# A windowed attention mixer in two-unit steps: keys' low halves laid out twice, weights divided by their sum before the transposes, two query chunks moved behind the values

## The chip, the core and the metric

One NeuronCore of a Trainium2 chip runs the kernel. TensorE (PE) multiplies, VectorE (DVE) and ScalarE (ACT) work elementwise and read the products from PSUM, GpSimd (POOL) works elementwise on SBUF and issues some of the transfers, SyncE (SP) issues the rest. The metric is the device time in microseconds of one execution, median of the runs.

## What is computed

Four layers with mixers A, B, C, A over 256 latent and 256 context tokens of width 1024, each mixer followed by a squared-ReLU MLP. The change is in mixer B, windowed grouped-query attention with 16 query heads, 4 key heads, head width 64. Latent queries see latent keys within 128 tokens and all context keys; context queries see context keys alone. The softmax has a learned sink logit per head:

```
def sink_softmax(scores, sink):
    m = sink
    for s in scores:
        m = jnp.maximum(m, jnp.max(s, axis=-1))
    ps = [jnp.exp(s - m[..., None]) for s in scores]
    denom = jnp.exp(sink - m)
    for p in ps:
        denom = denom + jnp.sum(p, axis=-1)
    return [p / denom[..., None] for p in ps]
```

## The kernel before

Activations are feature-major, eight chunks of 128 features by 512 tokens (latent first), in `h`, and split for matmuls into a high and a low half, `xh` and `xl`. Weights come as 374 blocks of 128x1024 in a fixed order; each is loaded by SP into a ring of four (`raw`), split by ACT (line 240) and DVE (line 245) into a ring of five (`hl`), and multiplied in three passes (`mm3`, lines 375 to 377). `w_get(ahead)` takes the next block and first queues the splits of the next `ahead` blocks on ACT and DVE. The order on every engine is that of the program text; the framework adds the waits.

Mixer B makes two key chunks and eight query chunks (`chunk`, `evac`, `put`, `rotate`), then the values for all heads (`v_step`, 256 columns, token-major), then attends. A unit is 128 queries of two heads (hh 0 and 1), that is a tuple (G, blk, j); there are 32, in groups of four (j) over blocks 0, 2, 1, 3: four latent units against 512 keys, four context units against 256, and so on. Latent units are called L, context units C below. A loop step `attend(x)` issues

- `s1(x)`: scores, two passes with the keys' high halves over 128 rows (line 1271), two with the low halves over 64 rows (line 1275), and for L a window mask of 256 columns per head (line 1278);
- `s4(x-2)`: transposes of the exponentials, 128x128 each (line 1331), and the copy to SBUF by ACT (line 1333), into `h`, whose contents are saved in DRAM meanwhile;
- `over_sum(x-2)`: a product of ones with a diagonal of the reciprocal sums (line 1352), which spreads them along a row;
- `pv(x-3)`: products with the values, two column halves of 64 (line 1343);
- `s2(x)`: row maxima (lines 1292, 1297), exponentials with row sums (line 1314), sums, reciprocals, diagonals.

At the end of a block `block_end` multiplies the outcome by the spread reciprocals (line 1364) and splits it into `xh`, `xl` (lines 1321, 1322). Eight output chunks follow: the first halves of chunks 0 and 1 are drawn into the last steps, 2 to 4 go through `chunk` with the default `ahead=4`, and 5 to 7 are the tail that `transition` multiplies between the mixer and the MLP (it takes their weights by `w_get(0)`). After each output chunk the residual is added (line 550) and its square taken for the norm (line 444).

Of the kernel before, what the change touches and what calls it, by code (L numbers as in the profile page):

```python
# [19 lines left out]
T = 256  # L20
DEPTH = 4
HID = 4096
NK = 8
# [52 lines left out]
def weight_order():  # L76

    order = []
    for l in range(DEPTH):
# [127 lines left out]
class Body:  # L207
# [968 lines left out]
    def mixer_b(self, l, i):  # L1176
        nc, tc = self.nc, self.tc
        with ExitStack() as st:
# [3 lines left out]
            KL = [bp.tile([128, 512], F32R, name=f"KL{G}") for G in range(2)]  # L1182
# [30 lines left out]
            def rotate(u, o):  # L1213
# [3 lines left out]
                def rest():  # L1217
                    rp = self.aux()[:, 0:T]
# [33 lines left out]
            S, P, PT, rsum, esum, diag = {}, {}, {}, {}, {}, {}  # L1252
            outs = [self.bank() for _ in range(4)]

            ring = [self.bank(), self.bank()]
            ring += [self.aux(), self.aux()]
            po, pr = outs[2], outs[3]
# [4 lines left out]
            def s1(x):  # L1262
# [5 lines left out]
                ss = [ring[2 * (x % 2) + hh] for hh in range(2)]  # L1268
                qs = Q2[G * 4 + j]
                for hh in range(2):  # L1270
                    nc.tensor.matmul(ss[hh][:, :nk], lhsT=qs[hh][:, ts_], rhs=K2[2 * G + hh][:, k0:512], start=True, stop=False)  # L1271

                for hh in range(2):
                    rows = slice(64 * hh, 64 * hh + 64)
                    nc.tensor.matmul(ss[hh][:, :nk], lhsT=qs[hh][rows, ts_], rhs=KL[G][rows, k0:512], start=False, stop=not lat)
                if lat:
                    for s in ss:
                        nc.tensor.matmul(
                            s[:, 0:T], lhsT=self.ident16, rhs=self.mask_w[:, blk * T : blk * T + T], start=False, stop=True
                        )  # L1280
                S[x] = [s[:, :nk] for s in ss]

            def s2(x):

                if x < N:
                    G, blk, j = units[x]
                    ci = G * 4 + j
                    nsk = self.nsinks[:, ci * 2 : ci * 2 + 2]
                    ngm = bq.tile([128, 2], F32, tag="ngm", name="ngm", bufs=4)
                    es = esum[x] = bq.tile([128, 2], F32, tag="es", name="es", bufs=4)  # L1290
                    rs = rsum[x] = bq.tile([128, 2], F32, tag="rs", name="rs", bufs=4)
                    nc.vector.tensor_reduce(ngm[:, 0:1], S[x][0], axis=AX.X, op=ALU.max, negate=True)
                old = rsum.get(x - 1)
                if x >= 1 and old is not None:
                    nc.vector.tensor_tensor(out=old, in0=old, in1=esum[x - 1], op=ALU.add)
                if x < N:
                    nc.vector.tensor_reduce(ngm[:, 1:2], S[x][1], axis=AX.X, op=ALU.max, negate=True)
                if old is not None:
                    nc.vector.reciprocal(old, old)
                if x < N:  # L1300
                    nc.vector.tensor_tensor(out=ngm, in0=ngm, in1=nsk, op=ALU.min)
                if old is not None:
                    diag[x - 1] = [bq.tile([128, 128], F32, tag="diag", name="diag", bufs=6) for _ in range(2)]
                    nc.vector.tensor_scalar(diag[x - 1][0], self.ident, old[:, 0:1], None, op0=ALU.mult)
                if x < N:
                    nc.vector.tensor_tensor(out=es, in0=ngm, in1=nsk, op=ALU.subtract)
                if old is not None:
                    nc.vector.tensor_scalar(diag[x - 1][1], self.ident, old[:, 1:2], None, op0=ALU.mult)
                if x < N:
                    P[x] = []  # L1310
                    for hh in range(2):
                        p = bq.tile([128, 512], F32, tag="p", name="p", bufs=6)
                        nk = S[x][hh].shape[-1]
                        nc.scalar.activation(
                            p[:, :nk], S[x][hh], AF.Exp, bias=ngm[:, hh : hh + 1], accum_out=rs[:, hh : hh + 1]
                        )
                        P[x].append(p[:, :nk])
                    nc.scalar.activation(es, es, AF.Exp)
                if block_done:
                    xh, xl, t = block_done.pop()  # L1320
                    nc.scalar.copy(xh, t)
                    nc.vector.tensor_tensor(out=xl, in0=t, in1=xh.bitcast(F32), op=ALU.subtract)

            def s4(x):
                G, blk, j = units[x]
                nkc = len(keys_of(blk)[0])
                PT[x] = []
                for hh in range(2):
                    tp = outs[hh].rearrange("p (c t) -> p c t", c=4)
                    for c in range(nkc):  # L1330
                        nc.tensor.transpose(tp[:, c, :], P[x][hh][:, c * 128 : c * 128 + 128], self.ident)  # L1331
                    t = self.h[:, 2 * (x % 4) + hh, :].rearrange("p (c t) -> p c t", c=4)
                    nc.scalar.copy(t[:, :nkc, :], tp[:, :nkc, :])
                    PT[x].append(t)

            def pv(x):
                G, blk, j = units[x]
                kcs = keys_of(blk)[0]
                js = slice(j * 128, j * 128 + 128)
                for c, kc in enumerate(kcs):  # L1340
                    for hh in range(2):
                        g = 2 * G + hh
                        nc.tensor.matmul(  # L1343
                            po[64 * hh : 64 * hh + 64, js], lhsT=vv[:, kc, g * 64 : g * 64 + 64], rhs=PT[x][hh][:, c, :],
# [3 lines left out]
            def over_sum(x):  # L1348

                j = units[x][2]  # L1350
                for hh in range(2):
                    nc.tensor.matmul(
                        pr[64 * hh : 64 * hh + 64, j * 128 : j * 128 + 128], lhsT=self.ones[:, 0:64], rhs=diag[x][hh],
                        start=True, stop=True,
                    )
# [379 lines left out]
```

## Time and profile before

| | |
|---|---|
| median of 3 runs | 2121.88 us (2120.83 to 2123.21) |
| profiled execution, its own time | 2119.28 us |
| its span, first to last instruction | 2117.4 us |
| PE busy | 2065.0 us, 98% |
| DVE, ACT, POOL busy | 1443.7, 950.7, 85.8 us |
| mean granted clock of PE | 0.993 |

A row of a timeline gives the start and the length of one instruction or of several merged ones. Matmuls are pipelined, so the length of one is longer than the distance to the next; what a group costs PE is read from the start of the next group. Mean durations of DVE and ACT are of single instructions.

### The profile page before, as it was taken

How to read it: one execution, taken by the hardware profiler on the slowest of the kernel's cores; microseconds unless marked ns; L12 is line 12 of the kernel's file. 1: busy time of each engine (PE TensorE's matmuls, PEld its weight loads, DVE VectorE, ACT ScalarE, POOL GpSimd, SP SyncE). 2: the span in 40 equal slices, each digit the busy share in tenths (PEclk: the TensorE clock that was granted, in tenths of full speed). 3: DMA queues.
4: the chain of work that ended last, by engine and by line, in shares of the span. 5: the costliest groups of instructions: out<-in, count | busy, mean ns of one | idle time of the engine just before them, and what ended most of it. 6: DMA issues, size and time to landing. Idle time of an engine off the chain costs nothing.

```text
span 2117.4 us, 30418 instructions
## 1 busy us (share of the span) xinstructions
PE 2065.0 (98%) x11782; PEld 1751.1 (83%) x11782; DVE 1443.7 (68%) x2636; ACT 950.7 (45%) x1818; POOL 85.8 (4%) x143
## 2 busy tenths in 40 slices
PE   6998999999999999999999999999999999989998
PEld 3667798888889877988888888898888889879997
DVE  5657777787767776677777664467777766577554
ACT  3426654324235585624234342362423435556554
POOL 0113100000000000000000000000000000310000
PEclk9999999999999999999999999999999999999999
DMA  9784235555553103255565333235556533635552
GB/s 297 266 283 113 75 128 174 186 189 179 188 171 118 52 1 130 90 189 180 180 197 177 122 110 100 90 110 189 183 179 195 181 110 110 174 98 186 182 185 92
DMA packets 97025, 326.11 MB, mean 154 GB/s; under 512 B 17760, under 2 KB 18928, under 8 KB 96240
## 3 DMA queue, kind: packets, MB, share of 16 engines
q1 hardware_dynamic: 80464, 291.19, 42.7%
q0 software_dynamic: 15872, 32.46, 5.0%
q8 instruction: 92, 1.51, 0.3%
q10 hardware_dynamic: 544, 0.52, 0.1%
q14 instruction: 53, 0.43, 0.1%
HBM read 319.73 MB, written 4.33 MB: 153 GB/s over the span
## 4 chain that ended last, share of the span: by engine, by line
PE 94%; DVE 3%; ACT 2%; DMA 1%; issue 1%; POOL 0%; DVEq 0%; SPq 0%; ACTq 0%
PE bank L375 25%; PE bank L377 25%; PE bank L376 25%; PE bank L576 2%; PE bank L577 2%; PE bank L579 2%; PE bank L407 2%; PE bank L409 1%; PE bank L408 1%; PE bank L291 1%; PE bank L1331 1%; PE bank L1343 1%; PE bank L1271 1%; DVE wlo L245 1%; ACT rb L942 1%; PE bank L1008 1%
## 5 line engine op out<-in xcount | busy, mean ns | idle before, releaser
L375 PE MATMUL bank<-xh,whi 128*128 128x512 f32 (+1 forms) x1600 | 578.8, 362 | 2.5 <-ACT h L895 1.8
L240 ACT CAST whi<-raw 128x1024 fp32r<-128x1024 f32 x374 | 387.1, 1044 | 419.9 <-PE bank L376 382.8
L376 PE MATMUL bank<-xl,whi 128*128 128x512 f32 (+1 forms) x1600 | 573.6, 358 | 0.2
L377 PE MATMUL bank<-xh,wlo 128*128 128x512 f32 (+1 forms) x1600 | 573.4, 358 | 0.0
L245 DVE TENSOR_TENSOR wlo<-raw,whi 128x1024 fp32r<-128x1024 f32 x374 | 454.8, 1223 | 165.6 <-ACT whi L240 165.0
L338 DVE SCALAR_TENSOR_TENSOR junk<-ada,cbc 128x1024 bf16<-128x1024 f32 x312 | 380.9, 1221 | 6.8 <-DMA ada<-in_ada 2.5
L375 PE MATMUL bank<-hh,whi 128*128 128x512 f32 (+1 forms) x1096 | 384.5, 351 | 0.0
L376 PE MATMUL bank<-hl,whi 128*128 128x512 f32 (+1 forms) x1096 | 383.9, 350 | 0.0
L377 PE MATMUL bank<-hh,wlo 128*128 128x512 f32 (+1 forms) x1096 | 383.9, 350 | 0.0
L375 PEld LDWEIGHTS bank<-xh,whi 128*128 128x128 f32 x1600 | 304.5, 190 | 53.3 <-issue 4.7
L376 PEld LDWEIGHTS bank<-xl,whi 128*128 128x128 f32 x1600 | 304.4, 190 | 43.8 <-DVE xl L928 1.0
L377 PEld LDWEIGHTS bank<-xh,wlo 128*128 128x128 f32 x1600 | 304.2, 190 | 44.0
L376 PEld LDWEIGHTS bank<-hl,whi 128*128 128x128 f32 x1096 | 207.4, 189 | 27.4
L375 PEld LDWEIGHTS bank<-hh,whi 128*128 128x128 f32 x1096 | 207.4, 189 | 27.3
L377 PEld LDWEIGHTS bank<-hh,wlo 128*128 128x128 f32 x1096 | 207.4, 189 | 27.0
L550 DVE SCALAR_TENSOR_TENSOR h<-bank,mod,h 128x256 f32<-128x256 f32 x280 | 125.6, 480 | 142.3 <-PE bank L377 142.2
L661 DVE TENSOR_TENSOR hl<-q,hh 128x512 fp32r<-128x512 f32 (+1 forms) x137 | 81.5, 595 | 170.4 <-ACT q L660 170.1
L658 ACT ACTIVATE r<-bank 128x512 f32<-128x512 f32 (+1 forms) x137 | 70.8, 517 | 268.9 <-PE bank L377 266.0
L444 ACT ACTIVATE sq<-h 128x256 f32<-128x256 f32 (+1 forms) x74 | 36.0, 487 | 140.9 <-DVE h L550 115.7
L576 PE MATMUL bank<-xh,whi 128*128 128x256 f32 x312 | 81.6, 290 | 3.5 <-ACT xh L512 3.5
L577 PE MATMUL bank<-xh,wlo 128*128 128x256 f32 x312 | 80.2, 285 | 0.0
L659 ACT ACTIVATE hh<-r 128x512 fp32r<-128x512 f32 (+1 forms) x137 | 75.9, 554 | 4.6
(269 smaller groups left out, 2144.0 us busy)
## 6 DMA issues: line engine op xcount, KB each, us to landing
raw<-in_wts SPq DMA_DIRECT2D x374, 512.0 KB, 4.2
ada<-in_ada SPq DMA_DIRECT2D x156, 512.0 KB, 3.5
first<-in_ada POOLq DMA_DIRECT2D x17, 512.0 KB, 5.1
start<-in_ada SPq DMA_DIRECT2D x16, 512.0 KB, 8.8
cbc<-line POOLq DMA_DIRECT2D x4, 1024.0 KB, 8.5
rb<-dnm POOLq DMA_DIRECT2D x16, 256.0 KB, 6.6
ab<-dar POOLq DMA_DIRECT2D x16, 256.0 KB, 10.8
h<-in_hin SPq DMA_DIRECT2D x4, 512.0 KB, 7.8
```

The source lines that it names most:

```text
L240: self.nc.scalar.copy(hi, self.raw[j])
L245: self.nc.vector.tensor_tensor(out=lo, in0=self.raw.pop(j), in1=hi.bitcast(F32), op=ALU.subtract)
L338: nc.vector.scalar_tensor_tensor(out=junk, in0=w, scalar=1.0, in1=self.cbc[:, s, :], op0=ALU.mult, op1=ALU.mult, accum_out=self.mods[l][:, ...
L375: mm(out, lhsT=whi, rhs=xhi, start=first, stop=False)
L376: mm(out, lhsT=whi, rhs=xlo, start=False, stop=False)
L377: mm(out, lhsT=wlo, rhs=xhi, start=False, stop=last)
L550: self.nc.vector.scalar_tensor_tensor(out=self.h[:, m, a:b], in0=o[:, a - sl.start : b - sl.start], scalar=mod[:, gate + m, s : s + 1], in ...
L576: mm(o[:, :T], lhsT=w[0][:, c], rhs=hi[:, sl], start=(k == 0), stop=False)
L577: mm(o[:, :T], lhsT=w[1][:, c], rhs=hi[:, sl], start=False, stop=False)
L658: nc.scalar.activation(r[:, :n], o, AF.Relu)
L659: nc.scalar.activation(hh[:, sl], r[:, :n], AF.Square)
L661: nc.vector.tensor_tensor(out=hl[:, sl], in0=q[:, :n], in1=hh[:, sl].bitcast(F32), op=ALU.subtract)
```

## The change

A loop step now holds two units of the same block, a pair `y` with units `2y` and `2y+1`, 16 pairs in all.

- The keys' low half lies at both halves of the rows (`KL[g]`), so that all score products use 128 rows. The mask is added on the 128 columns where it isn't zero.
- `maxima` takes both heads of a unit in one reduction; the sink's term is made once for a pair.
- `normalise` adds the sums, takes reciprocals, and has GpSimd multiply the exponentials by them, in place, ahead of the transposes. The diagonals, `over_sum` and the multiplication in `block_end` are gone.
- `turn` transposes with a ring of three banks; of an L unit ACT copies head 0 and DVE head 1, of a C unit DVE copies both at once.
- `pv` multiplies the values with both units of a pair, 256 columns.
- Query chunks 8 and 9 are multiplied behind the values, one before the loop and one in its step 1.
- Five output chunks instead of two have their first halves in the last steps, their second halves follow, and the tail of three is handed on at once. `h` comes back in two transfers.

The bodies that go stand in the listing above and are left out of the diff, as are lines that only move:

```diff
-            order += [("colq", "b_w_qkv", i, m) for m in range(8)]
+            order += [("colq", "b_w_qkv", i, m) for m in range(6)]
             order += [("mov", "b_w_qkv", i, 1280, 256, kk) for kk in range(2)]
+            order += [("colq", "b_w_qkv", i, m) for m in range(6, 8)]
             order += [("rowq", "b_w_out", i, m) for m in range(8)]
...
-            KL = [bp.tile([128, 512], F32R, name=f"KL{G}") for G in range(2)]
+            KL = [bp.tile([128, 512], F32R, name=f"KL{g}") for g in range(4)]
...
                     if u < 2:
                         hi = K2[2 * u + hh]
-                        lo = KL[u][rows, sl]
+                        lo = KL[2 * u + hh]
                         nc.scalar.copy(hi[away, sl], src[rows])
+                        parts.append((rows, hi[rows, sl], lo[rows, sl]))
+                        parts.append((rows, hi[rows, sl], lo[away, sl]))
                     else:
-                        lo = hi[away, sl]
+                        parts.append((rows, hi[rows, sl], hi[away, sl]))
                     nc.scalar.activation(hi[rows, sl], src[rows], AF.Copy, scale=scale)
-                    parts.append((rows, hi[rows, sl], lo))
...
-                def rest():
-                    rp = self.aux()[:, 0:T]
+                def rest(bank=None):
+                    rp = (self.aux() if bank is None else bank)[:, 0:T]
...
-            for u in range(3, 10):
+            for u in range(3, 8):
                 self.chunk(u, self.x_chunk, ALL, evac)
...
+            N = len(units) // 2
+            bk = self.banks
+            tring, po = [bk[2], bk[4], bk[3]], bk[5]
+            S, P, sums = {}, {}, {}
+            tpos = [0]
...
                 nk = 512 - k0
                 ts_ = slice(blk * 128, blk * 128 + 128)
                 lat = blk < 2
+                at = 6 * (x % 2)
+                ss = self.allb[:, at : at + 2, 0:nk]
                 qs = Q2[G * 4 + j]
                 for hh in range(2):
+                    g = 2 * G + hh
+                    nc.tensor.matmul(ss[:, hh, :], lhsT=qs[hh][:, ts_], rhs=K2[g][:, k0:512], start=True, stop=False)
+                    nc.tensor.matmul(ss[:, hh, :], lhsT=qs[hh][:, ts_], rhs=KL[g][:, k0:512], start=False, stop=not lat)
+                if lat:
+                    c = (1 - blk) * 128
+                    for hh in range(2):
+                        nc.tensor.matmul(
+                            ss[:, hh, c : c + 128], lhsT=self.ident16, rhs=self.mask_w[:, blk * T + c : blk * T + c + 128],
+                            start=False, stop=True,
+                        )
+                S[x] = ss
+            def maxima(x):
+                G, blk, j = units[x]
+                y, a = divmod(x, 2)
+                if a == 0:
+                    sums[y] = [bq.tile([128, 4], F32, tag=t, name=t, bufs=4) for t in ("ngm", "es", "rs")]
+                ngm = sums[y][0]
+                c = slice(2 * a, 2 * a + 2)
+                ci = G * 4 + j
+                nc.vector.tensor_reduce(ngm[:, c], S[x], axis=AX.X, op=ALU.max, negate=True)
+                nc.vector.tensor_tensor(out=ngm[:, c], in0=ngm[:, c], in1=self.nsinks[:, 2 * ci : 2 * ci + 2], op=ALU.min)
+                if a == 1:
+                    nc.vector.tensor_tensor(
+                        out=sums[y][1], in0=ngm, in1=self.nsinks[:, 2 * ci - 2 : 2 * ci + 2], op=ALU.subtract
+                    )
+            def exps(x):
+                y, a = divmod(x, 2)
+                ngm, es, rs = sums[y]
+                P[x] = []
                 for hh in range(2):
+                    p = bq.tile([128, 512], F32, tag="p", name="p", bufs=8)
+                    nk = S[x].shape[-1]
+                    at = 2 * a + hh
+                    nc.scalar.activation(
+                        p[:, :nk], S[x][:, hh, :], AF.Exp, bias=ngm[:, at : at + 1], accum_out=rs[:, at : at + 1]
+                    )
+                    P[x].append(p[:, :nk])
+                if a == 1:
+                    nc.scalar.activation(es, es, AF.Exp)
+            def normalise(y):
+                ngm, es, rs = sums.pop(y)
+                nc.vector.tensor_tensor(out=rs, in0=rs, in1=es, op=ALU.add)
+                nc.vector.reciprocal(rs, rs)
+                for a in range(2):
                     for hh in range(2):
+                        p = P[2 * y + a][hh]
+                        nc.gpsimd.tensor_scalar(p, p, rs[:, 2 * a + hh : 2 * a + hh + 1], None, op0=ALU.mult)
+            def turn(x):
+                nk = len(keys_of(units[x][1])[0]) * 128
+                at = 2 * (x % 4)
+                ps = P.pop(x)
+                if nk == 512:
+                    for hh in range(2):
+                        tp = tring[tpos[0] % 3]
+                        tpos[0] += 1
+                        for c in range(0, nk, 128):
+                            nc.tensor.transpose(tp[:, c : c + 128], ps[hh][:, c : c + 128], self.ident)
+                        if hh == 0:
+                            nc.scalar.copy(self.h[:, at, :], tp)
+                        else:
+                            nc.vector.tensor_copy(self.h[:, at + 1, :], tp)
+                else:
+                    tp = tring[tpos[0] % 3].rearrange("p (a k) -> p a k", a=2)
+                    tpos[0] += 1
+                    for hh in range(2):
+                        for c in range(0, nk, 128):
+                            nc.tensor.transpose(tp[:, hh, c : c + 128], ps[hh][:, c : c + 128], self.ident)
+                    nc.vector.tensor_copy(self.h[:, at : at + 2, 0:nk], tp)
+            def pv(y):
+                G, blk, j = units[2 * y]
                 kcs = keys_of(blk)[0]
+                at = 4 * (y % 2)
                 for c, kc in enumerate(kcs):
                     for hh in range(2):
                         g = 2 * G + hh
                         nc.tensor.matmul(
+                            po[64 * hh : 64 * hh + 64, j * 128 : j * 128 + 256], lhsT=vv[:, kc, g * 64 : g * 64 + 64],
+                            rhs=self.h[:, at + hh : at + hh + 3 : 2, c * 128 : c * 128 + 128],
                             start=(c == 0), stop=(c == len(kcs) - 1),
                         )
+            def block_end(y):
+                G, blk, _ = units[2 * y]
+                sl, cs = slice(blk * 128, blk * 128 + 128), slice(G * 4, G * 4 + 4)
+                t = po.rearrange("p (j t) -> p j t", j=4)
+                nc.scalar.copy(self.xh[:, cs, sl], t)
+                nc.vector.tensor_tensor(out=self.xl[:, cs, sl], in0=t, in1=self.xh[:, cs, sl].bitcast(F32), op=ALU.subtract)
+            early = []
+            def begin(o):
+                early.append((self.w_get(-1), o))
+                self.unit(o, early[-1][0], self.x_chunk, ALL, range(4))
+            def query(u, o, between, ahead):
+                w = self.w_get(ahead)
+                self.unit(o, w, self.x_chunk, ALL, range(4))
+                between()
+                self.unit(o, w, self.x_chunk, ALL, range(4, NK))
+                evac(u, o, ALL)
+            vo = [bk[j] for j in (5, 4, 3, 2)]
             for kk in range(2):
                 w = self.w_get(3 - kk)
                 for kx in range(4):
+                    self.v_step(w, 4 * kk + kx, vo, 256)
                     if pend and kx in (0, 2):
                         pend.pop(0)()
                     if kk == 1 and kx % 2 == 1:
                         s1(kx // 2)
             for tcn in range(4):
+                nc.scalar.copy(vv[:, tcn, :], vo[tcn][:, 0:256])
             for x in range(2):
+                maxima(x)
+                exps(x)
+            query(8, bk[5], lambda: None, 2)
+            for y in range(1, N + 3):
+                if y >= 5 and y % 2 == 1:
+                    block_end(y - 4)
+                t = 2 * (y - 2)
+                if 2 <= y < N + 2:
+                    turn(t)
+                if y < N:
+                    s1(2 * y)
+                    maxima(2 * y)
+                if y <= N:
+                    normalise(y - 1)
+                if y == 1:
+                    query(9, bk[4], lambda: pend.pop(0)(bk[2]), 3)
+                if y == 2:
+                    pend.pop(0)(bk[3])
+                if y in (N, N + 1):
+                    begin(bk[6 * (y - N)])
+                if 2 <= y < N + 2:
+                    turn(t + 1)
+                if y < N:
+                    exps(2 * y)
+                    s1(2 * y + 1)
+                    maxima(2 * y + 1)
+                    exps(2 * y + 1)
+                if y in (N, N + 1):
+                    begin(bk[6 * (y - N) + 1])
+                if y >= 3:
+                    pv(y - 3)
+                if y in (N - 3, N - 1):
                     self.wsplit_to(self.wsplit + 1)
+                if y > N:
+                    c = slice(4 * (y - N - 1), 4 * (y - N - 1) + 4)
+                    nc.gpsimd.dma_start(out=self.h[:, c, :], in_=saved[:, c, :])
+            begin(bk[2])
+            block_end(N - 1)
         res = self.residual(l, 16, 512)
         for m, (w, o) in enumerate(early):
             self.unit(o, w, self.x_chunk, ALL, range(4, NK))
             res(m, o, ALL)
+        self.bpos = 3
         yield self.x_chunk, res, (5, 6, 7)
```

## Rows read from the trace of the kernel before

**Rows 1.** The page's part 4, the chain that ended last, by engine

```profile
PE 94%; DVE 3%; ACT 2%; DMA 1%; issue 1%; POOL 0%; DVEq 0%; SPq 0%; ACTq 0%
```

**Rows 2.** PE in order of time: start us, us, engine, line, tiles, count

```profile
742.11 0.66 PE L1331 MATMUL bank<-cons,p 128*128 128x128 f32 x4
...
742.97 0.61 PE L1343 MATMUL bank<-h,vv 128*64 128x128 f32 x8
743.51 0.73 PE L1271 MATMUL bank<-K,Q 128*128 128x512 f32 x2
...
751.91 0.73 PE L1271 MATMUL bank<-K,Q 128*128 128x512 f32 x2
...
753.01 0.39 PE L1278 MATMUL bank<-mask_w,ident 128*128 128x256 bf16 x2
753.24 1.04 PE L1331 MATMUL bank<-cons,p 128*128 128x128 f32 x8
754.21 0.44 PE L1352 MATMUL bank<-diag,ones 128*64 128x128 f32 x4
754.48 1.04 PE L1343 MATMUL bank<-h,vv 128*64 128x128 f32 x16
755.45 0.51 PE L1271 MATMUL bank<-K,Q 128*128 128x256 f32 x2
...
756.20 1.09 PE L1331 MATMUL bank<-cons,p 128*128 128x128 f32 x8
...
766.20 0.73 PE L1271 MATMUL bank<-K,Q 128*128 128x512 f32 x2
```

**Rows 3.** PE in order of time, where the transition follows the output chunks

```profile
843.37 0.39 PE L377 MATMUL bank<-xh,wlo 128*128 128x512 f32 x1
843.59 0.28 PE L375 MATMUL bank<-xh,whi 128*128 128x256 f32 x1
843.71 0.28 PE L376 MATMUL bank<-xl,whi 128*128 128x256 f32 x1
```

**Rows 4.** Groups by line and form, 716 to 822 us: count | busy us, mean ns | idle before

```profile
L1314 ACT ACTIVATE p<-bank,ngm 128x512 f32<-128x512 f32 x32 | 21.7, 683 | 6.2 <-DVE ngm L1301 5.1
L1333 ACT COPY h<-bank 128x512 f32<-128x512 f32 x32 | 17.1, 592 | 0.6 <-PE bank L1331 0.6
L1314 ACT ACTIVATE p<-bank,ngm 128x256 f32<-128x256 f32 x32 | 15.0, 478 | 3.1 <-DVE ngm L1301 2.3
L1292 DVE TENSOR_REDUCE ngm<-bank 128x1 f32<-128x512 f32 x16 | 11.0, 687 | 3.1 <-PE bank L1278 3.1
L1292 DVE TENSOR_REDUCE ngm<-bank 128x1 f32<-128x256 f32 x16 | 6.8, 423 | 6.1 <-PE bank L1275 5.7
```

**Rows 5.** DVE and ACT in order of time: the hand-over to an exponential

```profile
746.99 0.16 DVE L1301 TENSOR_TENSOR ngm<-ngm,nsinks 128x2 f32<-128x2 f32 x1
...
747.24 0.69 ACT L1314 ACTIVATE p<-bank,ngm 128x512 f32<-128x512 f32 x1 [1.34 <-DVE ngm L1301]
```

**Rows 6.** POOL and DVE in order of time, in mixer A of layer 0

```profile
156.87 1.29 POOL L875 TENSOR_TENSOR ab<-ab,qT 128x512 f32<-128x512 f32 x1
...
177.83 1.60 POOL L875 TENSOR_TENSOR ab<-ab,qT 128x512 f32<-128x512 f32 x1
...
177.62 0.68 DVE L901 SCALAR_TENSOR_TENSOR h<-h,ssum 128x512 f32<-128x512 f32 x1
178.34 1.65 DVE L902 SCALAR_TENSOR_TENSOR h<-h,ssum 128x512 f32<-128x512 f32 x1
```

**Rows 7.** Groups of POOL, whole span, shapes apart

```profile
L806 POOL MEMSET wrow<- 40x512 f32 x2 | 1.2, 594 | 0.0
```

**Rows 8.** The page's part 5, costliest groups of the whole span

```profile
L240 ACT CAST whi<-raw 128x1024 fp32r<-128x1024 f32 x374 | 387.1, 1044 | 419.9 <-PE bank L376 382.8
...
L245 DVE TENSOR_TENSOR wlo<-raw,whi 128x1024 fp32r<-128x1024 f32 x374 | 454.8, 1223 | 165.6 <-ACT whi L240 165.0
...
L550 DVE SCALAR_TENSOR_TENSOR h<-bank,mod,h 128x256 f32<-128x256 f32 x280 | 125.6, 480 | 142.3 <-PE bank L377 142.2
```

More of the change, by code (lines that the diff above doesn't have):

```diff
@@ L1267, in s1 @@
                 lat = blk < 2
-                ss = [ring[2 * (x % 2) + hh] for hh in range(2)]
+                at = 6 * (x % 2)
+                ss = self.allb[:, at : at + 2, 0:nk]
                 qs = Q2[G * 4 + j]
                 for hh in range(2):
-                    nc.tensor.matmul(ss[hh][:, :nk], lhsT=qs[hh][:, ts_], rhs=K2[2 * G + hh][:, k0:512], start=True, stop=False)
-                for hh in range(2):
-                    rows = slice(64 * hh, 64 * hh + 64)
-                    nc.tensor.matmul(ss[hh][:, :nk], lhsT=qs[hh][rows, ts_], rhs=KL[G][rows, k0:512], start=False, stop=not lat)
@@ L1276, in s1 @@
[L1276 to L1310, printed above, removed]
-                    for hh in range(2):
[L1312 to L1334, printed above, removed]
@@ L1343, in pv @@
                         nc.tensor.matmul(
-                            po[64 * hh : 64 * hh + 64, js], lhsT=vv[:, kc, g * 64 : g * 64 + 64], rhs=PT[x][hh][:, c, :],
+                            po[64 * hh : 64 * hh + 64, j * 128 : j * 128 + 256], lhsT=vv[:, kc, g * 64 : g * 64 + 64],
+                            rhs=self.h[:, at + hh : at + hh + 3 : 2, c * 128 : c * 128 + 128],
                             start=(c == 0), stop=(c == len(kcs) - 1),
                         )
[L1348 to L1355, printed above, removed]
-                if j == 3:
-                    t = bq.tile([128, 512], F32, tag="on", name="on", bufs=2)
-                    nc.scalar.copy(t, pr)
-                    over.append(t)
@@ L1361, in block_end @@
-            def block_end(G, blk):
-                sl = slice(blk * 128, blk * 128 + 128)
-                t = over.pop()
-                nc.vector.tensor_tensor(out=t, in0=po, in1=t, op=ALU.mult)
-                cs = slice(G * 4, G * 4 + 4)
-                block_done.append((self.xh[:, cs, sl], self.xl[:, cs, sl], t.rearrange("p (j t) -> p j t", j=4)))
-            N = len(units)
-            over, block_done, early = [], [], []
-            def attend(x):
-                if x >= 7 and x % 4 == 3:
-                    block_end(*units[x - 4][:2])
-                if x < N:
-                    s1(x)
-                if 2 <= x < N + 2:
-                    s4(x - 2)
-                    over_sum(x - 2)
-                if 3 <= x < N + 3:
-                    pv(x - 3)
-                s2(x)
+            def block_end(y):
[4 more added lines that the diff above has]
+                nc.vector.tensor_tensor(out=self.xl[:, cs, sl], in0=t, in1=self.xh[:, cs, sl].bitcast(F32), op=ALU.subtract)
@@ L1391, in mixer_b @@
             for tcn in range(4):
-                nc.scalar.copy(vv[:, tcn, :], outs[tcn][:, 0:256])
+                nc.scalar.copy(vv[:, tcn, :], vo[tcn][:, 0:256])
             for x in range(2):
-                s2(x)
-            for x in range(2, N + 4):
-                attend(x)
-                if x in (N, N + 2):
-                    self.wsplit_to(self.wsplit + 1)
-                if x in (N + 1, N + 2):
-                    early.append((self.w_get(-1), ring[x - N - 1]))
-                    self.unit(early[-1][1], early[-1][0], self.x_chunk, ALL, range(4))
-            for c in range(0, 8, 2):
-                nc.gpsimd.dma_start(out=self.h[:, c : c + 2, :], in_=saved[:, c : c + 2, :])
+                maxima(x)
[30 more added lines that the diff above has]
+                if y in (N - 3, N - 1):
+                    self.wsplit_to(self.wsplit + 1)
+                if y > N:
[3 more added lines that the diff above has]
+            block_end(N - 1)
         res = self.residual(l, 16, 512)
@@ L1408, in mixer_b @@
             res(m, o, ALL)
-        for m in range(2, 5):
-            self.chunk(m, self.x_chunk, ALL, res)
+        self.bpos = 3
         yield self.x_chunk, res, (5, 6, 7)
```

9 lines of the change are left out of this document (removed).

## The prediction

> **What bounds the kernel now.** I read the chain that ended last first: 94% of it is PE [rows 1], so what PE is given to do counts, and so does each moment in which it has to wait. Then PE's timeline inside mixer B [rows 2]. The distance from one group's start to the next is its price. An L unit: scores 1.33 us (751.91 to 753.24, of which the mask pair is 0.23), eight transposes 0.97, the spread sums 0.27, values 0.97; in all 3.54. A C unit: scores 0.75 (755.45 to 756.20), four transposes and spread sums together 0.86 (742.11 to 742.97), so 0.59 for the transposes, values 0.54; in all 2.15. Four of each are 22.8, and the trace has 22.7 from one block of L units to the next (743.51 to 766.20): no time is lost in a round, PE sets its pace, and there are four rounds. Last, the groups of DVE and ACT in that stretch [rows 4], for what each step costs on the engines that must follow.
>
> **The change, PE's work first.** A pass of 512 columns on the whole array is 0.22, one of 256 is 0.12 [rows 3]. New scores of an L unit are four passes and half the mask, 0.88 + 0.12 = 1.0, of a C unit 4 x 0.12 = 0.48. Transposes stay, 0.97 and half of that, 0.49. The spread sums go. Value products are half as many with twice the columns: at most what they were, 1.94 for an L pair and 1.08 for a C pair; at least half of that, if columns cost nothing. I take the first, since columns are what PE streams in rows 3. So an L pair is 2 x 1.0 + 2 x 0.97 + 1.94 = 5.9 instead of 7.1, a C pair 0.96 + 0.98 + 1.08 = 3.0 instead of 4.3, a round 17.8 instead of 22.7. Over four rounds PE has 19.6 less to do (27 with the other end of the value price).
>
> **Whether PE can run at 17.8.** A round asks 17.8 of DVE and 13.6 of ACT by the prices below, so at best DVE just keeps up. And each engine takes its instructions in order, so I followed the order. DVE prices: a reduction is 0.69 for 512 columns and 0.42 for 256, so 1.22 for the 1024 that two heads now are; a copy of 512 columns from PSUM or the subtraction of `block_end` the same 0.69; a [128,2] operation 0.16 [rows 5]. ACT: a copy 0.59, exponentials of a unit 2 x 0.68 or 2 x 0.48 [rows 4]; a hand-over to ACT 0.1 (746.99 + 0.16 to 747.24) [rows 5]. From PE to a reader I take 0.2, the 0.28 of a matmul less the 0.12 between two [rows 3]. One round, from the last exponential of step 4 to that of step 8:
>
> - Step 5 (second L pair, C transposes): ACT's cast of `block_end` stands behind the exponentials of step 4, DVE's subtraction waits for it and stands first on DVE. 0.59 + 0.69, copy 0.69, maxima 1.38, sum and reciprocal 0.32, copy 0.69, maxima 1.38, hand-over 0.1, exponentials 1.36: 7.2.
> - Step 6 (C scores, L transposes): three banks take four transposes, so the last waits for ACT's copy of the first, and that copy is behind step 5's exponentials. Copy 0.59, transposes 0.49, scores 0.48, 0.2, maxima 0.85, 0.1, exponentials 0.96: 3.7.
> - Steps 7 and 8: cast 0.59, copy 0.59 and the transposes that wait for its bank 0.49, scores 0.48, values 1.94, next transposes 0.49, L scores 1.0, 0.2, maxima 1.38, sum and reciprocal 0.32, copy 0.69, maxima 1.38, 0.1, exponentials 1.36: 11.0.
>
> That is 21.9 a round, with PE waiting 4.1 of it; DVE and ACT then hold most of the gain. Against 22.7 it saves 0.8, and over 3.5 rounds (the first half round is the filling) 2.8.
>
> **GpSimd's products.** Four per pair; the trace has no product with a scalar there. Below it costs the 0.59 of a fill of 512 columns that reads nothing [rows 7], above the 1.29 of a product with two inputs [rows 6]; it reads one tensor, so I take the middle, 0.9. In step 5 the sums are ready some 3.5 into the 7.2; two products end 1.8 later, before the bank is free, and the fourth at 7.1, just before it is wanted. At 0.9 the price is nothing and the cover is that bank wait; at 1.29 the fourth comes 1.5 later, and step 7 meets the same again: up to 2 a round. The page "GPSIMD Engine Reference" of the Trainium skill, on the side-by-side cycle accounting, has 769 ns for 512 elements in its best loop with one input; by that figure the sum would be the same and the slow GpSimd below less likely. No row here shows it.
>
> **A port that two engines share.** Alone, DVE's operation on two SBUF tensors took 0.68; the next of that shape took 1.65, and a POOL product ran from 177.83 to 179.43, 0.56 ahead of DVE's end at 179.99 [rows 6], so DVE's own work began when the product was done. So they exclude each other. The new `min` and `subtract` on `ngm` and `nsinks` read two SBUF tensors, and the `min` of the second unit of each step falls among the four products. Waiting half a product each time costs 2 x 0.45 for L products and 2 x 0.25 for C: 1.4 a round at most, none if so small an operation slips in or the wait is off the chain. Behind the waiting `min` stand the exponentials, for which the scores' banks and the next sums wait. I take half, 0.7 a round, 2.5 in all. The Trainium skill, "SBUF — State Buffer", section Who interferes with whom, says that the shared pair is an exclusive lock and that the loser blocks for the whole instruction; the trace agrees with 1.65 against 0.68. By the rule the sum would be 2.4 higher, without it 2.5 lower.
>
> **Filling.** Query chunk 9 is evacuated on ACT ahead of the exponentials of unit 2, and its rotation is put into the bank that unit 1's transposes want, with DVE's read behind sums that wait for unit 3's exponentials. I count 4.5 of PE waiting in steps 2 and 3. Half a round of the work removed (2.4) and the old filling and draining waits, which five output halves now cover, go against it: 0 in the sum, -2 to +3.
>
> **The split in step 13.** `wsplit_to` puts a cast of 1.04 on ACT and a subtraction of 1.22 on DVE [rows 8], between the step's exponentials and the copies of L transposes of step 14. DVE waits there for the cast. Both lie on the chain: 2.3, and 2.9 with the fourth GpSimd product late; I take 2.5. If the chain has slack, 0. The one in step 15 meets output products that cover it.
>
> **The tail.** Before, PE went from the output chunks into the transition without a gap (843.37, 843.59, 843.71) [rows 3], since chunks 2 to 4 had queued the splits of 5 to 7. Now no `w_get` between step 15 and the transition splits ahead, and ACT and DVE take the split of output block 5 behind the residual and square of chunk 4. After its last matmul: 0.2, two residuals 0.96, a square 0.6 (as an ACT pass of 512), cast 1.04, subtraction 1.22: 4.0 during which PE has at most two passes to do. Nothing covers it.
>
> **Costed at nothing.** The moved query chunks are the same 48 passes of 512 each. The keys' second low half is eight more DVE passes of 0.42 under query products; 3.4 without that cover. The mask on fewer columns is in the scores. The return of `h` is issued a step before its first reader, with half chunks of 12 x 0.22 = 2.6 between; it comes into the tail's wait one for one if it lands later than three of them. SP's queue has loaded its four blocks long before, and the moved blocks keep their order there.
>
> **Sum.** -2.8 + 2.5 + 0 + 2.5 + 4.0 = +6.2. On the profiled execution's 2119.3 that is 2125.5; the median of the runs lies 2.6 above that, so 2128.
>
> **Rivals.**
> - *PE keeps its pace of 17.8.* Decided where the chain of steps 5 to 8 takes less than 17.8 instead of 21.9. For it: the sums of DVE and ACT would just allow it, and a chain worked out by hand is easily too long by a hand-over here and there. Against: the order of the text makes step 5's chain, and three banks make step 6's. Then -19.6, the split covered, the tail paid: -15.6, 2106. Half way between, 20 a round: -9.5 + 1 + 2.5 + 4.0 = -2, and -5.5 without port waits and split (2116).
> - *It cancels.* No port waits and a chain shorter by 1: 6.2 - 2.5 - 3.5 = 0, 2122. Nothing in the trace excludes it; both terms are estimates.
> - *GpSimd is slow.* Products at 1.29 add 2 a round: +7, 2135; with the port held from one product to the next, a `min` waits for several: up to 2142. For it: the one product that the trace has costs 1.29; against: it reads twice as much.
>
> **How the numbers follow.** About 0.2% (4.2) is what a measurement here can tell from no change. Forecast (+4.2 to +13): 0.37. Slow GpSimd: 0.14. Cancels, -4.2 to +4.2: 0.23. PE at its pace or half way: 0.26. So slower 0.51, same 0.23, faster 0.26. The range leaves out the full pace at the one end (about 0.1) and the worst of GpSimd at the other: 2109 to 2139; the likeliest case alone is 2125 to 2134.
>
> **What would show it.** Right, if a round of eight units is 21 to 23.5 long with PE waiting several us in it, on banks that ACT's copies free and on GpSimd's products; if `min` of [128,2] has long instances beside GpSimd's products; if PE stands still about 4 before the transition, behind a cast and a subtraction. Wrong, if rounds are near 18, if GpSimd's product is over 1.2 or under 0.6, or if score passes over 128 rows with repeated weights don't come at 0.22.

## The result, and the profile after

The changed kernel takes 2146.12 us (median of 4 runs, 2141.96 to 2148.44) against 2122.55 of the kernel before (4 runs): 1.0109 times, 95% interval [1.0097, 1.0122], some 23.6 us slower. Forecast were 2128, within 2109 to 2139: the sign held, the size didn't. The profiled execution is the slowest of the four (2148.44; span 2146.7). The chain that ended last, from its page, answers to [rows 1], with GpSimd's product on it. The last line is that product's group, two shapes mixed:

```profile
PE 89%; DVE 5%; ACT 2%; POOL 2%; issue 1%; DMA 1%; SPq 0%; DVEq 0%; ACTq 0%; POOLq 0%
PE bank L376 24%; PE bank L378 24%; PE bank L377 24%; POOL p L1326 2%; PE bank L577 2%; PE bank L578 2%; PE bank L580 2%; PE bank L408 2%; PE bank L410 1%; PE bank L409 1%; PE bank L292 1%; DVE wlo L246 1%; ACT rb L943 1%; PE bank L1009 1%; PE bank L1358 1%
...
L1326 POOL TENSOR_SCALAR p<-p,rs 128x512 f32<-128x512 f32 (+1 forms) x64 | 81.7, 1293 | 100.3 <-PE bank L378 75.3
```

PE in order of time, after: landmarks and some of the waits between them. The landmarks are the first rotation, v (the values), the first scores, the L scores with which rounds 2 to 4 begin, the first output pass, the transition and its sum of squares. In brackets stands how long PE had waited, and for what:

```profile
680.37 1.02 PE L1221 MATMUL bank<-qr,cons 128*128 128x256 f32 x4
...
704.75 0.47 PE L408 MATMUL bank<-whi,xh 128*128 128x256 f32 x1
...
709.48 0.35 PE L408 MATMUL bank<-whi,xh 128*128 128x256 f32 x1 [4.02 <-DVE Q L1211]
...
720.21 0.40 PE L1275 MATMUL bank<-K,Q 128*128 128x512 f32 x1
...
754.65 0.47 PE L1275 MATMUL bank<-K,Q 128*128 128x512 f32 x1
...
766.53 0.66 PE L1338 MATMUL bank<-cons,p 128*128 128x128 f32 x4 [2.37 <-POOL p L1326]
768.07 1.12 PE L1338 MATMUL bank<-cons,p 128*128 128x128 f32 x4 [0.89 <-POOL p L1326]
...
781.09 0.47 PE L1275 MATMUL bank<-K,Q 128*128 128x512 f32 x1
...
807.11 0.47 PE L1275 MATMUL bank<-K,Q 128*128 128x512 f32 x1
...
834.39 0.47 PE L376 MATMUL bank<-xh,whi 128*128 128x512 f32 x1
...
870.08 0.43 PE L376 MATMUL bank<-xh,whi 128*128 128x256 f32 x1 [2.61 <-ACT whi L241]
...
871.34 0.58 PE L378 MATMUL bank<-xh,wlo 128*128 128x256 f32 x1 [0.62 <-DVE wlo L246]
...
884.15 0.61 PE L451 MATMUL bank<-ssum,ones 128*128 128x256 f32 x2
```

The same landmarks before, as far as [rows 2, 3] don't have them:

```profile
674.71 1.03 PE L1219 MATMUL bank<-qr,cons 128*128 128x256 f32 x4
...
710.95 0.47 PE L407 MATMUL bank<-whi,xh 128*128 128x256 f32 x1
...
720.61 0.63 PE L1271 MATMUL bank<-K,Q 128*128 128x512 f32 x2
...
788.89 0.73 PE L1271 MATMUL bank<-K,Q 128*128 128x512 f32 x2
...
815.41 0.50 PE L375 MATMUL bank<-xh,whi 128*128 128x512 f32 x1
...
854.02 0.61 PE L450 MATMUL bank<-ssum,ones 128*128 128x256 f32 x2
```

Their differences, us:

| stretch | before | after | difference |
|---|---|---|---|
| first rotation to v | 36.24 | 24.38 | -11.86 (two query chunks moved) |
| v to first scores | 9.66 | 15.46 | +5.8 |
| first round | 22.90 | 34.44 | +11.54, so -0.3 without the moved chunks |
| rounds 2 and 3 | 45.38 | 52.46 | +7.1 |
| round 4 to first output pass | 26.52 | 27.28 | +0.8 |
| to the transition | 28.18 | 35.69 | +7.5 (the draining now lies in here) |
| transition to its sum of squares | 10.43 | 14.07 | +3.6 |
| sum, "mixer B" below | 179.31 | 203.78 | +24.5 |

The last stretch scatters by 1.1. Nine of the kernels of this study, the changed one among them, have the same code from the first output pass on; seven of their traces take 13.0 there, this one and that of `by_one` 14.1 and 14.2, with the same waits but a mean granted clock of 0.76 instead of 0.87. The 5.66 by which this execution reached mixer B later are scatter too: in the 14 profiles of this study, with the same code ahead, the first rotation starts at 673.94 to 680.67. So each kernel below has its ratio to the kernel before and mixer B's length in its trace.

GpSimd's products after (groups by form, 735 to 835 us: count | busy, mean ns | idle before):

```profile
L1326 POOL TENSOR_SCALAR p<-p,rs 128x512 f32<-128x512 f32 x32 | 52.6, 1661 | 87.8 <-PE bank L378 75.3 <-DVE rs L1322 10.8 <-ACT h L1340 1.7
L1326 POOL TENSOR_SCALAR p<-p,rs 128x256 f32<-128x256 f32 x28 | 25.4, 925 | 9.6 <-DVE rs L1322 8.5 <-PE bank L1276 1.1
```

The term had 0.9 and 0.5. Four in a row take 6.19 (from 771.49), more than the 5.9 that PE was to need for an L pair. The mean of 1661 ns hides two cases: 28 of the 32 products took 1.55 to 1.57, and four took 3.41, 2.39, 1.82 and 1.76. All four ran beside a DVE operation with two inputs in SBUF. The longest two began while DVE split a weight block (1.23 alone); below are one of them, each instruction by itself, and a small DVE operation beside an ordinary product:

```profile
821.73 1.23 DVE L246 TENSOR_TENSOR wlo<-raw,whi 128x1024 fp32r<-128x1024 f32 x1 [2.12 <-ACT whi L241]
821.99 2.39 POOL L1326 TENSOR_SCALAR p<-p,rs 128x512 f32<-128x512 f32 x1
...
773.03 1.56 POOL L1326 TENSOR_SCALAR p<-p,rs 128x512 f32<-128x512 f32 x1
773.28 0.46 DVE L1297 TENSOR_TENSOR ngm<-ngm,nsinks 128x2 f32<-128x2 f32 x1
```

Windows of after, around v's start and the transition; the third column from the right is the granted clock:

```profile
core 0: us, PE busy (x) PEld busy (x) DVE busy (x) ACT busy (x) POOL busy (x), PEclk, DMA share, GB/s
704.00:709.60 5.60, 1.58 (x9) 1.23 (x9) 4.33 (x10) 2.90 (x6) 0.00 (x0) 1.00 0.35 98
709.60:713.40 3.80, 3.80 (x18) 3.62 (x19) 2.83 (x8) 0.83 (x2) 0.00 (x0) 0.55 0.39 132
...
866.00:870.40 4.40, 1.79 (x9) 1.21 (x7) 2.60 (x5) 2.32 (x4) 0.00 (x0) 0.99 0.00 0
870.40:877.20 6.80, 6.18 (x29) 5.89 (x29) 5.35 (x5) 3.51 (x4) 0.00 (x0) 0.51 0.64 195
```

Behind the long waits PE worked at its lower level (0.5 is 1.2 GHz), so a wait can cost more than its own length. The sum had no term for that.

### The profile page after: what moved, and what is told of

Its sections match the earlier page's. It is cut to its first block, busy times and chain, and to the rows that moved or that the text cites. A ratio compares the mean times of both kernels' runs of the same rounds, so it can differ in the third digit from the quotient of the medians.

```text
span 2146.7 us, 29755 instructions
## 1 busy us (share of the span) xinstructions
PE 2064.4 (96%) x11462; PEld 1747.4 (81%) x11462; DVE 1449.8 (68%) x2524; ACT 928.7 (43%) x1746; POOL 166.6 (8%) x205
## 4 chain that ended last, share of the span: by engine, by line
PE 89%; DVE 5%; ACT 2%; POOL 2%; issue 1%; DMA 1%; SPq 0%; DVEq 0%; ACTq 0%; POOLq 0%
PE bank L376 24%; PE bank L378 24%; PE bank L377 24%; POOL p L1326 2%; PE bank L577 2%; PE bank L578 2%; PE bank L580 2%; PE bank L408 2%; PE bank L410 1%; PE bank L409 1%; PE bank L292 1%; DVE wlo L246 1%; ACT rb L943 1%; PE bank L1009 1%; PE bank L1358 1%
## 5 line engine op out<-in xcount | busy, mean ns | idle before, releaser
L1326 POOL TENSOR_SCALAR p<-p,rs 128x512 f32<-128x512 f32 (+1 forms) x64 | 81.7, 1293 | 100.3 <-PE bank L378 75.3
```

The source lines that it names most:

```text
L1326: nc.gpsimd.tensor_scalar(p, p, rs[:, 2 * a + hh : 2 * a + hh + 1], None, op0=ALU.mult)
```

## The experiments

All start from the changed kernel, `b_keys` from the kernel before. There are three suspects: GpSimd's product, the wait in v, the wait at the transition. Each outcome gives the median, its ratio to the kernel before with a 95% interval, the length of mixer B in the trace, and, where they bear on it, the lengths of rounds 2 and 3 (before 22.7, after 26.4 and 26.0).

**undivided.** The product in `normalise` is left out.

> The changed kernel without GpSimd's four products a pair: the weights reach the transposes undivided, so the output isn't the reference's. Theory 1, GpSimd's product (1.66 us for 512 columns, where 0.9 was in the sum) sets the pace: a round falls from 26.4 us to the 21.9 that the chain of ACT and DVE was worked out to, 3.5 rounds give 16, and with the drops of PE's clock that go with the long waits the time is 2125 to 2131. Theory 2, the chain of ACT and DVE is as slow by itself and the products only end last: 2140 or more. Theory 3, PE keeps its own 17.8 a round once the products are gone: 2116 or less.

2132.29 us, ratio 1.0053 [1.0038, 1.0068], mixer B 191.98. PE in order of time:

```profile
750.58 0.47 PE L1275 MATMUL bank<-K,Q 128*128 128x512 f32 x1
...
764.75 0.66 PE L1338 MATMUL bank<-cons,p 128*128 128x128 f32 x4 [1.82 <-ACT h L1340]
...
773.51 0.47 PE L1275 MATMUL bank<-K,Q 128*128 128x512 f32 x1
...
795.52 0.47 PE L1275 MATMUL bank<-K,Q 128*128 128x512 f32 x1
```

Rounds of 22.9 and 22.0: the chain of ACT and DVE, worked out as 21.9, is what is left. It fits step by step: between the last exponentials, steps 5, 6 and 7 with 8 took 7.0, 4.1 and 11.9 us, a round later 7.0, 4.0 and 11.0, for 7.2, 3.7 and 11.0 worked out. The longest wait is the one of step 6, the bank that ACT's copy frees. Theory 1, though a little above its time. Mixer B is 11.8 shorter; 1.0 of that is the scatter of the last stretch, so the products cost 10.8 of the 24.5. Even without them the kernel is slower than before.

**by_one.** `tensor_scalar(p, p, 1.0, ...)` in place of `rs[...]`.

> The changed kernel with GpSimd's product kept, but by the constant 1.0 instead of by a column of 1/sum, so that the weights stay undivided and the output isn't the reference's. If the price of GpSimd's product is its pass over 512 columns of f32 in SBUF: the same 1.55 to 1.66 us, the time within 3 of the changed kernel's 2146. If it is the scalar that is read from a column: 0.8 us or less, rounds near the 22.0 to 22.9 without products, 2130 to 2134.

2136.38 us, 1.0079 [1.0064, 1.0094], mixer B 194.06, rounds of 23.0 and 23.1. Groups of POOL, 735 to 830 us:

```profile
L1326 POOL TENSOR_SCALAR p<-p 128x512 f32<-128x512 f32 x28 | 41.5, 1510 | 18.7 <-ACT p L1311 18.7
L1326 POOL TENSOR_SCALAR p<-p 128x256 f32<-128x256 f32 x32 | 26.5, 848 | 8.2 <-ACT p L1311 8.0
```

By single instructions, 30 of the 32 products of 512 columns took 1.48 to 1.51 (median 1.49), against a median of 1.56 with the column: the pass is the price, the column of scalars adds 0.07. Yet the rounds are short and the time is 10 below the 2146 of the first expectation: these products don't wait for sums, each starts behind its exponential. So it is a slow product and a late start together: four products that may begin only when DVE has added a whole pair's sums.

**diag.** The division in the transposes: `matmul(tp, lhsT=p, rhs=diag)` for `transpose(tp, p, ident)`, four diagonals a pair on DVE.

> The changed kernel with the division moved into the transposes: DVE writes four 128x128 diagonals of 1/sum a pair (into the old mask tile and a scratch tile) and PE multiplies each block of weights by its diagonal instead of by the identity; GpSimd does nothing. Theory 1 (GpSimd's product sets the pace): as without the products, plus up to 4 x 0.16 of DVE a pair, 2126 to 2135. Theory 2 (the chain of ACT and DVE is the bound): no better than 2145, since DVE gets more work. Rival: a matmul by a diagonal is dearer than a transposition and takes the gain back.

2150.93 us, 1.0143 [1.0128, 1.0159], mixer B 208.17, rounds of 26.1. The time fits theory 2 as well, but PE was busy for 23.8 of each round at a granted clock of 1.00, so it is the rival that held. Groups of PE, 752 to 805 us (two rounds):

```profile
L1338 PE MATMUL bank<-mw,p 128*128 128x128 f32 x64 | 8.5, 281 | 4.5 <-ACT h L1342 2.5 <-DVE mw L1325 2.1
L1338 PE MATMUL bank<-sq,p 128*128 128x128 f32 x64 | 8.0, 278 | 0.0
```

Eight L units take 64 transpositions in two rounds (the changed kernel's group of that line has x64 there), but 128 matmuls by a diagonal: two instructions and 0.22 us a block (eight blocks from 771.40 to 773.20 in this trace), against one and 0.12 for a transposition ([rows 2], 753.24 to 754.21). That and four diagonals on DVE (0.87 a pair) eat the gain.

**share.** Of a pair's four products two stay on GpSimd, one goes to DVE, one to ACT.

> The changed kernel with a pair's four products shared out: two stay on GpSimd (3.1 us a pair instead of 6.2), one goes to DVE behind the reciprocal, one to ACT behind the first unit's exponentials. Theory: GpSimd's four in a row behind late sums set the 26.4; with two the chain of ACT and DVE ends last again, 22.0 a round as without products, longer by the product on DVE (some 0.4) in each of its steps: 23 to 24 a round and 2135 to 2139. Rival: DVE and ACT have no room, or DVE's product waits for GpSimd's at the shared port: 25 a round or more, 2142 or more.

2138.70 us, 1.0072 [1.0057, 1.0087], mixer B 196.92, rounds of 23.3 and 23.9: as worked out.

**order.** `block_end` behind the next maxima, `s1(2y + 1)` ahead of `turn(t + 1)`.

> The changed kernel with the same operations in another order: a block's split into xh and xl behind the next maxima instead of ahead of the step, and the second unit's scores ahead of the second unit's transposes. GpSimd keeps its four products. If GpSimd's rate alone sets the pace, a round can't go under 2 x 6.2 + 2 x 3.7 = 19.8, and earlier sums bring it to 21 to 24: 2130 to 2140. If the chain behind the sums is what counts, nothing moves: 25.5 or more a round, 2144 or more.

2141.22 us, 1.0087 [1.0070, 1.0104], mixer B 198.90, rounds of 24.45: between the two. The order alone saves some 1.8 a round with GpSimd's load unchanged.

**vbanks.** v's first weight goes to three free banks for all four k, then to the bank of query chunk 7:

```
-vo = [bk[j] for j in (5, 4, 3, 2)]
+vo = [bk[j] for j in (5, 2, 3, 4)]     # kk = 0: tcn 0 to 2 for kx 0 to 3, then tcn 3
```

> The changed kernel with the order of v's first weight alone changed: its four steps go to three banks first and to query chunk 7's bank last, so that 4.1 us of v's products lie ahead of the bank that PE waited 4.02 us for. Theory A, that wait and the half clock behind it (3.4 us at half, at most 1.7 lost) are a price of the moved query chunks: 2140 to 2142. Theory B, the work behind v waits for query chunk 7 anyway, so that the time only moves: 2145 or more.

2140.41 us, 1.0090 [1.0072, 1.0108], mixer B 198.23. From v to the first scores it takes 11.07 instead of 15.46, and the clock doesn't drop there. Theory A, with 4.4 of the 5.8. The 1.4 that is left is mostly a wait of 1.18 for DVE in a query chunk's rotation.

**splits.** `if m < 3: self.wsplit_to(self.wsplit + 1)` behind `res(m, o, ALL)` of the early output chunks.

> The changed kernel with the splits of output blocks 5 to 7 put behind the residuals of output chunks 0 to 2. Theory A, the 2.6 and 0.6 us that PE stands still ahead of the transition, and the 6.8 us at half clock behind them (at most 3.4 lost), come from the split of block 5 behind chunk 4's residual: 2139.5 to 2143. Theory B, ACT and DVE have no room for the splits under the output halves and the wait returns one residual later: 2145 or more.

2139.35 us, 1.0087 [1.0069, 1.0106], mixer B 198.70. The first output pass to the transition takes 32.91 instead of 35.69, the rest 11.68 instead of 14.07. Theory A: wait and clock are 5.2 together, or 4.1 by the 13.0 of most traces. A new wait of 1.10 ahead of the sum of squares stays.

**q_ahead.** Query chunks 8 and 9 ahead of v again, in the weights' order too.

> The changed kernel with query chunks 8 and 9 back ahead of v, and one split put into step 2. Theory A, the moved chunks cover the filling (the first round took 34.4 with 11.9 of query products in it, so 22.5 of its own against 26.4 later): without them PE waits through the first pair's maxima, exponentials and four products, some 10 us, and the wait ahead of v (5.7 with its clock) goes: 2147 to 2153. Theory B, the move costs its wait and brings nothing: 2139 to 2142.

2143.75 us, 1.0110 [1.0093, 1.0127], mixer B 200.55. The wait in v is gone, and the first round is 25.84 instead of 34.44 - 11.86 = 22.58. The moved chunks cost 5.8 and covered at most 3.3 of filling, for this run also puts one split into step 2. The time is between the two theories, nearer to B, and in the ratio there is no difference from the changed kernel that could be measured.

**warm.** Matmuls without a reader in the waits ahead of v and of each L block's first transposes.

> The changed kernel with matmuls that nobody reads: 18 of 512 columns ahead of v's first product and 10 ahead of the first L transposes of a block, where PE waits 4.0 and 2.4 us. The waits stay, PE is busy in them. Theory clock: the granted clock's drops at those five places cost up to 1.7 us for each 3.4 at half; without them 2139 to 2143. Theory waits alone: the drops lie beside GpSimd's products and cost nothing, 2145 to 2150.

2141.92 us, 1.0107 [1.0092, 1.0122], mixer B 200.64. From the first rotation to the first scores it takes 38.25 instead of 39.84, so 1.6 of v's price is the clock; rounds of 25.99, 26.00 and 27.26 instead of 26.44, 26.02 and 27.28, so in the rounds the clock costs at most 0.5. In the whole time the difference is not to be told from none.

**b_keys.** In the kernel before, the keys' second low half and the narrow mask alone.

> The kernel before with one part of the change alone: the keys' low half laid out twice and the mask on its own 128 columns (its diagonals lie in the old mask tile and a scratch tile to make room). PE bounds it and a unit's scores fall from 1.33 to 1.03 us (L) and by as much or less (C), so a round loses 1.2 to 2.3 of 22.7: 2112 to 2117 where PE keeps its pace. Rival: ACT or DVE of the old order can't follow (they are some 3 us below PE's round), 2119 to 2122.

2118.75 us, 0.9986 [0.9977, 0.9996], mixer B 175.94, rounds of 21.5 and 21.9: 3.4 shorter in the trace, and PE waits 0.4 in all three rounds. The rounds lose 0.8 to 1.2, so 2112 to 2117 was missed by 2, though PE kept its pace. This part only takes work from the engine that is the bound, and it pays; no other part was tried alone in the kernel before.

**tuned.** `share`, `order`, `vbanks` and `splits` together.

> The three findings together: products shared as two on GpSimd, one on DVE, one on ACT; the order with the split behind the maxima and the second scores ahead of the second transposes; v's first weight on the three free banks first; the splits of output blocks 5 to 7 behind the residuals. If the terms add: 5.7 for v, 6.8 for the tail, and rounds of 19 to 21 instead of 26.4 (PE alone needs 17.8), so 2108 to 2118, below both kernels. If the rounds stay at 22 or more: 2119 to 2124.

2120.89 us, 0.9994 [0.9984, 1.0004], mixer B 179.96. PE in order of time, one round:

```profile
769.81 0.48 PE L1275 MATMUL bank<-K,Q 128*128 128x512 f32 x1
...
778.29 1.08 PE L1363 MATMUL bank<-h,vv 128*64 128x256 f32 x8 [0.57 <-DVE xl L1374]
...
780.52 0.66 PE L1343 MATMUL bank<-cons,p 128*128 128x128 f32 x4 [0.56 <-POOL p L1327]
...
787.91 1.95 PE L1363 MATMUL bank<-h,vv 128*64 128x256 f32 x16 [0.41 <-DVE xl L1374]
...
790.20 0.48 PE L1275 MATMUL bank<-K,Q 128*128 128x512 f32 x1
```

A round of 20.39 with 1.54 of waiting at a granted clock of 1.00, so PE's own round is 18.85, not 17.8. The rounds came out as expected and the time did not: 2108 to 2118 was missed. Measured singly in mixer B, with the last stretch's clock counted once, the four edits save 19.2, together 23.8, so they do add. But that only leads back to the kernel before: 2.3 are saved in each of rounds 2 and 3, and given back in v (1.4), in the first round (35.92 - 11.86 against 22.90, 1.2) and from round 4 to the sum of squares (67.82 against 65.13, 2.7).

**tuned2.** Ring of banks 2, 3, 4; two splits earlier; one copy from DVE to ACT.

> The last version with three more edits for what its trace shows: the ring of the transposes' banks as 2, 3, 4, so that the second transpose of the first unit doesn't wait for query chunk 9's bank (1.20 and 3.06 us there, and 10.2 us at half clock around them); the splits of output blocks 1 and 2 taken ahead with query chunk 8 instead of 9; the first C unit's copy on ACT instead of DVE, which was busy nearly throughout the steps with L scores. If the waits in the first round and DVE set the time that is left: the first round 4 to 8 shorter, later rounds 19 to 20 instead of 20.4, 2110 to 2116. If ACT becomes late instead, or the wait goes to the next bank: 2119 to 2122.

2120.17 us, 0.9991 [0.9982, 1.0000], mixer B 178.74. The first round is 2.3 shorter, rounds 2 and 3 are 20.39 again, so DVE's copy was not what set them; the expected gain isn't there. From round 4 to the sum of squares it takes 68.95, 3.8 more than before and 1.1 more than `tuned`. Those 1.1 lie in round 4 and are the clock: PE waits less there (3.9 against 4.3), but the granted clock is 0.93 instead of 1.00.

## Why the prediction was wrong

- **Right: PE's work.** L scores took 1.03 among v's products (720.21 to 721.24) and 1.11 in a round (769.81 to 770.92 in `tuned`), 1.0 forecast; an L pair's values 1.88 (757.39 to 759.27), 1.94 forecast. PE's own round is 1 longer than its sum.
- **Right: the chain.** 21.9 forecast, 22.0 and 22.9 in `undivided`, and the steps fit too; so PE could not keep 17.8 in this order, and that rival fell.
- **Failed: GpSimd's product, the step that decided.** 0.9 was taken, with 1.29 as the upper end because one input should cost no more than two. It costs 1.56, 1.66 on average; the argument from the count of inputs was no row, and it is false here, since the product with two inputs takes 1.29. The 1.60 of [rows 6] would have been a better upper end, but by luck: that product ran beside two DVE operations on SBUF, and the other five of its shape up to 200 us took 1.27 to 1.31. So the price wasn't to be read from the trace, and the range had to allow for that. At 0.9 the product was hidden at no price; the rival "GpSimd is slow" had the mechanism, with up to 2 a round. It is 3.5 and 4.0 (26.4 and 26.0 against 22.9 and 22.0), 10.8 in all. The Trainium skill's "GPSIMD Engine Reference", on the side-by-side cycle accounting, has 769 ns for 512 elements in its best loop. This instruction takes 1490 to 1560 where nothing delays it, and the measurement decides.
- **Failed: "the moved query chunks are the same 48 passes", at nothing.** The passes are; what they covered isn't. Query chunk 7's evacuation was hidden by chunks 8 and 9, and v's second bank is chunk 7's. The price is 5.8, of which `vbanks` takes back 4.4 by the order of the banks alone. I looked for the missing cover in the steps that got the chunks, not where they had left. The filling itself was right: 0 forecast, -0.3 measured, with waits of 1.6 and 2.3 for the query chunks' evacuation and rotation where 4.5 were counted.
- **Nearly right: the tail.** The place and the two instructions were right (cast, then subtraction). The waits are 2.61 and 0.62 instead of 4.0; with the lower clock behind them, which the sum left out, they cost 5.2 in this trace and 4.1 by most others. That the sum comes near 4.0 is in part luck.
- **Small, and not where it was sought: the port and the split.** Groups of DVE, 735 to 835 us after, then 735 to 822 us in `undivided`:

```profile
L1297 DVE TENSOR_TENSOR ngm<-ngm,nsinks 128x2 f32<-128x2 f32 x29 | 5.6, 192 | 1.0
...
L1299 DVE TENSOR_TENSOR es<-ngm,nsinks 128x4 f32<-128x4 f32 x15 | 3.6, 238 | 0.5
```

```profile
L1297 DVE TENSOR_TENSOR ngm<-ngm,nsinks 128x2 f32<-128x2 f32 x29 | 4.7, 161 | 1.0
...
L1299 DVE TENSOR_TENSOR es<-ngm,nsinks 128x4 f32<-128x4 f32 x15 | 2.4, 163 | 0.5
```

Beside GpSimd's products they take 29 x 31 ns + 15 x 75 ns = 2.0 us more in all, on the chain or off it (2.5 forecast). The same sharing cost GpSimd more: the four long products lost 3.1, and the sum had nothing for that. The reading behind the term was loose, too, for the operation of 0.68 in [rows 6] wasn't alone: the product had begun 0.21 behind it. The split of step 13 is in round 4: 27.28 against 26.2 for the mean of rounds 2 and 3, so 1.1; without products, 25.1 against 22.5, so 2.6 (2.5 forecast). No run leaves that split out, so its price isn't shown.

Taken singly and with the last stretch's clock counted once, products 10.8, v 4.4 and tail 5.2 make 20.4 of the 24.5. The other 4.1 no run takes out by itself; 1.4 of it is left in v.

## What to carry to other kernels

Before work is moved, write down what it hides at the place that it leaves, bank by bank, as well as what it will hide where it goes. The price of an operation that the trace doesn't hold is open upwards, so let the range reach beyond the nearest rows, and where several such operations stand in a row behind one late value, multiply and compare with the step. If PE sets the pace, first make the edit that only takes passes from it.

## What the runs showed of the hardware

- A product of 128x512 f32 by a scalar took GpSimd 1.49 us with a constant (`by_one`) and 1.56 with a column, DVE 0.49 and ACT 0.72 (both in `tuned`).
- A wait of 4.02 us was followed by a granted clock of 0.55 for 3.8 us, and waits of 2.61 and 0.62 by 0.51 for 6.8. The Trainium skill, "TensorE: Matmul & The Clock Gate", What's actually happening, says that an idle PE falls back to the lower level, and these rows agree.
- GpSimd's products and DVE's operations with two inputs in SBUF delay each other. A product that began 0.26 behind a split of 1.23 on DVE took 2.39 instead of 1.56, so 0.8 more, with 1.0 of the split to go. A DVE operation of [128,2] beside a product took 0.19 us on average instead of 0.16, one of [128,4] 0.24, and 0.52 at most; that of 773.28 ended 0.85 ahead of the product that had begun before it. The Trainium skill, "SBUF — State Buffer", Who interferes with whom, states an exclusive lock for the whole instruction. The product beside the split comes near that; the small operations don't fit it.
- An f32 matmul by a diagonal took two instructions and 0.22 us for a block of 128x128, a transposition one and 0.12.
